# Second block: gate and heads copied out of PSUM by ACT, norm scales in the rotary tables, routing rows rounded in natural order

## The chip, the cores and the metric

The kernel runs on one core of one Trainium2 chip. A core has TensorE (PE, matrix products into PSUM), VectorE (DVE), ScalarE (ACT), GpSimd (POOL) and SyncE (SP, which here only issues DMAs); each works through its own instructions in order and waits on semaphores for the others. The metric is the device time of one execution in microseconds; for the kernel before it is the median of three runs.

## The reference

The function runs two transformer blocks on T = 256 tokens of width 1024, all in fp32. The first block has a feed-forward, a mixer of two attentions, a second feed-forward and a gated embedding stage. The second block, in which the change lies, is this (normalisations take a gain vector):

```python
h = rmsnorm(x, attn_norm)
q, k, v, iq, ik, iw, z, xbc, dt_raw, gate_a, gate_b = split(h @ w_in)
q = rope_partial(rmsnorm(q by 16 heads of 64, q_norm), pos)   # rope on the first 16 of 64 dims
k = rope_partial(rmsnorm(k by 4 heads of 64, k_norm), pos)
y_attn = dsa_attention(q, k, v, iq, ik, iw)                   # top-k of an index score, then softmax
xs, bs, cs = split(silu(causal_depthwise_conv(xbc)))
y_ssd = ssd_chunked(xs, dt, A, bs, cs) + d_skip * xs
y_ssd = gated_group_rmsnorm(y_ssd, z, ssd_norm)               # y * silu(z), then a norm by group
x = x + (sigmoid(gate_a) * (y_attn @ w_a) + sigmoid(gate_b) * (y_ssd @ w_s)) @ w_out
x = x + hier_moe(rmsnorm(x, ffn_norm))                        # 4 groups of 8 experts, two used per token
```

`rmsnorm(q, g)` is q times the reciprocal root of its mean square, times g. `rope_partial` rotates dims 0 to 7 against 8 to 15 with cos and sin and leaves 16 to 63 as they are.

## The kernel before

**Products.** An fp32 product is made of three products of rounded parts: hi by hi, hi by lo, lo by hi. Every chunk of weights comes as `raw` (1 MB DMAs from SP, four buffers), ACT rounds it to `hi` (L211) and DVE takes `lo` = raw - hi (L212); five pairs of hi and lo fit. So SP's DMAs wait for `lo` of an older chunk, ACT and DVE for a free pair, that is for PE, and PE for `lo`. PSUM has banks under the names `mm` (3), `o` (1), `at` (2) and `tp` (2); who reads a bank last decides when PE may write it again.

**Order.** The order of each engine's instructions is found when the program is built, by a list scheduler, except where the code says `keep`; POOL's is as written. On the chip each engine follows its list and cannot go round a wait.

**Second feed-forward (from about 405 to 575 us).** The input's norm is applied late: `by_token` (L398) makes two diagonal matrices of the tokens' scales (`diag`, L403, DVE), and PE's L404 multiplies them with a matrix of -1 to get the scales as a row, which DVE multiplies into the gate's half `sa` (L430). Products of this stage are L302 and L303. In the same stretch POOL issues the small DMAs of block 2's constants (`block2_consts`, lines 865 ff., helper L136 for a vector broadcast to all partitions) and of the routing (L1326 to L1335); DVE's L1400 multiplies a gain into the routing weights.

**Block 2 (from about 625 us).** `w_in`'s columns come by chunks in an order that weaves the gate `z`, the queries and `xbc` together. Queries and keys go through `heads_of`: DVE multiplies the PSUM bank by the broadcast gain into `q` or `k` (L954), ACT squares the bank (L956), DVE sums (L958), POOL takes the power -1/2 (L145) and DVE a Newton step (L153 to L156: `u`, `r`). Then DVE applies rope (L502 to L505) and PE transposes (L513). The gate's bank is read by ACT's tanh (L1242) and then by DVE, (tanh + 1) * z (L1243). DVE also runs the top-k on index scores in the same stretch (L1005 to L1019), and ACT the scores' relu (`rel`, L1002).

**End.** From about 972 us on SP streams 96 MB of expert weights (L1381, order kept) into 32 buffers and more of 512 KB, which become free as earlier stages finish; routing (`Route.feed`) runs meanwhile, and its rows are gathered per expert by products with a permutation matrix (L1465) that read the rounded rows `hfh` and `hfl` as weights.

## Time and profile before

| | us |
|---|---|
| median of three runs | 1232.69 (1232.3 to 1237.01) |
| the profiled execution | 1233.61 |
| its span | 1231.9 |
| PE busy | 1158.9 (94%) |
| DVE busy | 765.7 (62%) |
| ACT busy | 580.9 (47%) |
| POOL busy | 82.2 (7%) |

The profile is of one execution; times in it count from the start of its span. Busy times of matmuls include their pipelining, so a busy PE is not PE at its peak. A row of a timeline gives start and length in us, engine, line, operation, the tiles written and read, and in brackets how long the engine had been idle and what released it.

### The profile page before, as it was taken

What the parts mean: (1) busy time and instruction counts of PE and PEld (TensorE: products, weight loads), DVE (VectorE), ACT (ScalarE), POOL (GpSimd) and SP (SyncE); (2) the same over time, 40 slices, a digit from 0 to 9 for tenths busy, and PEclk for the clock granted to TensorE, in tenths of its full rate; (3) what the DMA queues carried; (4) which work ended last, traced back from release to release, by engine and by line L of the source; (5) the groups of instructions that cost most, each with busy time, mean ns of one, the idle gap of its engine ahead of it and who ended that gap; (6) DMA issues with size and microseconds to landing.
All of it is one profiled execution on the core that took longest, in us unless ns stands there. A gap on an engine that the chain in (4) does not pass through costs nothing.

```text
span 1231.9 us, 18388 instructions
## 1 busy us (share of the span) xinstructions
PE 1158.9 (94%) x7126; PEld 908.0 (74%) x7127; DVE 765.7 (62%) x1407; ACT 580.9 (47%) x947; POOL 82.2 (7%) x144
## 2 busy tenths in 40 slices
PE   6999999999999999999998899999999999787776
PEld 5888888977778788888876788898787875342432
DVE  6676748776447677664788777799786662121213
ACT  6555535456565556553654476666544431010100
POOL 2000001110000500000010200001010010000000
PEclk9999999999999999999999899999999999999999
DMA  9554754563334765475542444334754699999996
GB/s 344 185 202 122 255 173 147 176 200 125 120 113 151 195 201 178 135 253 199 176 169 71 171 138 138 137 103 141 188 184 155 220 416 418 418 417 419 418 419 252
DMA packets 106827, 266.23 MB, mean 216 GB/s; under 512 B 8692, under 2 KB 18592, under 8 KB 106736
## 3 DMA queue, kind: packets, MB, share of 16 engines
q1 hardware_dynamic: 104000, 259.45, 59.0%
q0 software_dynamic: 1728, 4.00, 1.4%
q10 hardware_dynamic: 1008, 1.57, 0.4%
q8 instruction: 57, 0.93, 0.3%
q14 instruction: 34, 0.28, 0.1%
HBM read 263.95 MB, written 1.05 MB: 215 GB/s over the span
## 4 chain that ended last, share of the span: by engine, by line
PE 55%; DMA 11%; DVE 8%; ACT 1%; POOL 1%; issue 1%; ACTq 0%; DVEq 0%; SPq 0%; POOLq 0%
PE mm L228 8%; PE mm L230 8%; PE mm L229 8%; DMA wq<-in_w_up_dram 4%; PE mm L302 3%; DMA wq<-in_w_gate_dram 2%; DVE lo L212 2%; PE at L302 2%; PE at L1579 2%; DMA wq<-in_w_down_dram 2%; PE mm L1632 2%; PE mm L1087 2%; PE mm L1088 1%; PE tp L302 1%; PE mm L1089 1%; PE mm L303 1%
## 5 line engine op out<-in xcount | busy, mean ns | idle before, releaser
L212 DVE TENSOR_TENSOR lo<-raw,hi 128x1024 fp32r<-128x1024 f32 (+3 forms) x312 | 366.0, 1180 | 179.5 <-ACT hi L211 175.0
L211 ACT CAST hi<-raw 128x1024 fp32r<-128x1024 f32 (+3 forms) x312 | 315.9, 1016 | 284.9 <-PE o L229 95.0
L302 PE MATMUL mm<-x,hi 128*128 128x512 f32 x272 | 100.4, 402 | 2.8 <-DVE x L184 2.8
L145 POOL TENSOR_TENSOR r<-ms,phalf 128x1 f32<-128x1 f32 (+2 forms) x40 | 40.9, 1024 | 723.3 <-DVE ms L143 718.1
L1579 PE MATMUL at<-wq,xg 128*32 128x256 f32 x736 | 66.9, 396 | 17.0 <-DMA wq<-in_w_up_dram 12.7
L228 PE MATMUL mm<-hi,xah 128*128 128x512 f32 x192 | 78.9, 412 | 2.6 <-DVE zs L1243 2.6
L303 PE MATMUL mm<-x,lo 128*128 128x256 f32 x272 | 76.5, 283 | 0.1
L229 PE MATMUL mm<-lo,xah 128*128 128x512 f32 x192 | 76.2, 397 | 0.2 <-DVE ms L143 0.2
L230 PE MATMUL mm<-hi,xal 128*128 128x512 f32 x192 | 76.1, 396 | 0.3 <-DVE xal L184 0.3
L302 PE MATMUL at<-x,hi 128*128 128x512 f32 x192 | 70.3, 392 | 0.0
L1579 PEld LDWEIGHTS at<-wq,xg 128*32 128x32 f32 x736 | 31.2, 112 | 46.4 <-DMA wq<-in_w_up_dram 23.0
L1589 DVE SCALAR_TENSOR_TENSOR act<-at,cg,sa 128x256 f32<-128x256 f32 x8 | 5.3, 665 | 94.3 <-ACT sa L1586 94.3
L302 PEld LDWEIGHTS mm<-x,hi 128*128 128x128 f32 x272 | 52.0, 192 | 15.3 <-DVE x L184 3.5
L1087 PE MATMUL mm<-xah,hi 128*128 128x256 f32 x192 | 57.7, 300 | 3.1 <-ACT sq L956 3.1
L302 PE MATMUL tp<-x,hi 128*128 128x512 f32 x160 | 59.0, 392 | 0.0
L1088 PE MATMUL mm<-xal,hi 128*128 128x256 f32 x192 | 55.9, 291 | 0.0
L1089 PE MATMUL mm<-xah,lo 128*128 128x256 f32 x192 | 55.4, 289 | 0.0
L1586 ACT ACTIVATE sa<-at,rs 128x256 f32<-128x256 f32 x8 | 3.8, 474 | 108.6 <-PE at L1579 74.4
L303 PE MATMUL at<-x,lo 128*128 128x256 f32 x192 | 53.5, 279 | 0.0
L303 PEld LDWEIGHTS mm<-x,lo 128*128 128x128 f32 x272 | 52.1, 193 | 0.8 <-DVE lo L212 0.8
L229 PE MATMUL mm<-lo,gxh 128*128 128x512 f32 x132 | 51.6, 391 | 0.0
L230 PE MATMUL mm<-hi,gxl 128*128 128x512 f32 x132 | 51.6, 391 | 0.0
(577 smaller groups left out, 2712.9 us busy)
## 6 DMA issues: line engine op xcount, KB each, us to landing
raw<-in_w_in_dram SPq DMA_DIRECT2D x50, 1024.0 KB, 4.9
raw<-in_ffn_w_in_dram SPq DMA_DIRECT2D x40, 1024.0 KB, 5.0
wq<-in_w_up_dram SPq DMA_DIRECT2D x48, 512.0 KB, 9.9
wq<-in_w_down_dram SPq DMA_DIRECT2D x48, 512.0 KB, 9.9
raw<-in_ffn_w_out_dram SPq DMA_DIRECT2D x22, 1024.0 KB, 5.0
wq<-in_w_gate_dram SPq DMA_DIRECT2D x44, 512.0 KB, 9.9
raw<-in_w_gate_dram SPq DMA_DIRECT2D x20, 512.0 KB, 10.0
raw<-in_w_out_dram SPq DMA_DIRECT2D x8, 1024.0 KB, 4.8
```

The costliest lines, as they stand in the source:

```text
L145: G.tensor_tensor(out=r0, in0=ms, in1=phalf[:, :n], op=ALU.pow)
L211: first(S.copy(hi, part))
L212: first(V.tensor_tensor(lo, part, hi.bitcast(F32), op=ALU.subtract))
L228: PE.matmul(ps, xh, wh, start=first, stop=False)
L229: PE.matmul(ps, xh, wl, start=False, stop=False)
L230: PE.matmul(ps, xl, wh, start=False, stop=last)
L302: PE.matmul(ps[f], hi[:, c, s], sx.both[k // 2][:, :, k % 2, :], start=(k == 0), stop=False)
L303: PE.matmul(ps[f][:, 1, :], lo[:, c, s], sx.hi(k), start=False, stop=(k == KC - 1))
L1087: PE.matmul(o, hi[:, c, s], xh, start=(k == 0 and f % 2 == 0), stop=False)
L1088: PE.matmul(o, hi[:, c, s], xl, start=False, stop=False)
L1089: PE.matmul(o, lo[:, c, s], xh, start=False, stop=(k == 7 and f % 2 == 1))
L1579: PE.matmul(pg[s, n * 256:n * 256 + 256], xg[k // 4][:, k % 4, c:c + CAP], ws[j][:, r * 256:r * 256 + 256], start=(n + k == 0), stop=(n + ...
```

## The change

1. `heads_of`: the multiplication by the gain (L954) goes. ACT copies the bank to `q` or `k` and then squares it; rope follows on the copy at once, with cos and sin tables that have the gain of the 16 rotated dims in them; the gain of the other 48 dims is applied by ACT when it takes the transposed heads out of PSUM, as a scale per partition (1 for the rotated dims).
2. The tables: eight products of 128x2x8 on DVE in the constants' second part. POOL's two broadcasts of 64 become two of 16 (`q_norm_rot`, `k_norm_rot`), two memsets and four DMAs of 48x1 (`..._rest`), all in the same place.
3. `on_z`: ACT copies the bank to `zs` and writes the tanh to a tile of its own; DVE's product reads both from SBUF.
4. `Route.feed`: the rows are rounded in natural order, one contiguous cast and one contiguous subtraction for each half of the tokens; PE then reads the gather's weights with a stride of eight elements. The first half's subtraction moves behind the permutation, as the second's was.

```diff
--- before.py
+++ after.py
...
-    def to_T(src, dst, n, width):
+    def to_T(src, dst, n, width, scale=None):
...
-            S.copy(dst[:width, j:j + m, :], p[:width, :m, :])
+            if scale is None:
+                S.copy(dst[:width, j:j + m, :], p[:width, :m, :])
+            else:
+                S.activation(dst[:width, j:j + m, :], p[:width, :m, :], AF.Identity, scale=scale[:width])
...
-        g_q = row_bcast(a["q_norm_2"], 64, "g_q2")
-        g_k = row_bcast(a["k_norm_2"], 64, "g_k2")
+
+        g_rot, g_rest = {}, {}
+        for nm in ("q_norm_2", "k_norm_2"):
+            g_rot[nm] = row_bcast(a[nm][:16], 16, nm + "_rot")
+            g_rest[nm] = cp.tile([128, 1], F32, name=nm + "_rest")
+            G.memset(g_rest[nm], 1.0)
+            for b in range(2):
+                G.dma_start(g_rest[nm][64 * b + 16:64 * b + 64, :], a[nm][16:64].rearrange("(p o) -> p o", o=1))
         g_ik = row_bcast(a["idx_k_norm_2"], 64, "g_ik2")
...
+        tabs = {}
+        for nm in g_rot:
+            c, n = [cp.tile([128, 2, 2, 8], F32, name=nm + z) for z in ("_c", "_s")]
+            g = g_rot[nm].rearrange("p (j d) -> p j d", j=2)
+            for j in range(2):
+                V.tensor_tensor(c[:, :, j], cs2[:, :, j], bc(g[:, None, j], [128, 2, 8]), op=ALU.mult)
+                V.tensor_tensor(n[:, :, j], sn2[:, :, j], bc(g[:, None, 1 - j], [128, 2, 8]), op=ALU.mult)
+            tabs[nm] = c, n, g_rest[nm]
+        g_q, g_k = tabs["q_norm_2"], tabs["k_norm_2"]
...
-        def heads_of(ps, n, gain, dst):
-
-            V.tensor_tensor(dst, ps.rearrange("p (h d) -> p h d", d=64), bc(gain[:, None, :], [128, n, 64]), op=ALU.mult)
+        def heads_of(ps, n, t, gain, dst):
+
+            S.copy(dst.rearrange("p h d -> p (h d)"), ps)
             sq = heap([128, n, 64], name="sq")
             S.activation(sq.rearrange("p h d -> p (h d)"), ps, AF.Square)
+            rope(dst[:, :, :16], gain[0][:, t], gain[1][:, t], n, 8)
             ss = small([128, n], name="ss")
             V.tensor_reduce(out=ss, in_=sq, axis=AX.X, op=ALU.add)
             return rstd(ss, n, 64)
...
-            rh = heads_of(ps[:, :256], 4, g_k, k)
-            rope(k[:, :, :16], cs2[:, t], sn2[:, t], 4, 8)
+            rh = heads_of(ps[:, :256], 4, t, g_k, k)
             kd = heap([128, 4, 2, 64], name="kd")
             V.tensor_tensor(kd, bc(k[:, :, None, :], [128, 4, 2, 64]), bc(rh[:, :, None, None], [128, 4, 2, 64]), op=ALU.mult)
-            defer(lambda: to_T(kd.rearrange("p h j d -> p (h j d)"), kT2[:, :, tok(t)], 4, 128), DEFK)
+            defer(lambda: to_T(kd.rearrange("p h j d -> p (h j d)"), kT2[:, :, tok(t)], 4, 128, g_k[2]), DEFK)
...
             q = heap([128, 8, 64], name="q2")
-            rh = heads_of(ps, 8, g_q, q)
+            rh = heads_of(ps, 8, t, g_q, q)
             V.tensor_scalar(sc_q[t][:, bi * 8:bi * 8 + 8], rh, 0.125, None, op0=ALU.mult)
-            rope(q[:, :, :16], cs2[:, t], sn2[:, t], 8, 8)
-            defer(lambda: to_T(q.rearrange("p h d -> p (h d)"), qT2[bi][:, :, tok(t)], 4, 128), DEFQ)
+            defer(lambda: to_T(q.rearrange("p h d -> p (h d)"), qT2[bi][:, :, tok(t)], 4, 128, g_q[2]), DEFQ)
...
         def on_z(t, bi, n0, nw, ps):
-            S.activation(zs[bi][:, t, :], ps, AF.Tanh, scale=0.5)
-            V.scalar_tensor_tensor(zs[bi][:, t, :], zs[bi][:, t, :], 1.0, ps, op0=ALU.add, op1=ALU.mult)
+            th = heap([128, 512], name="zth")
+            S.copy(zs[bi][:, t, :], ps)
+            S.activation(th, ps, AF.Tanh, scale=0.5)
+            V.scalar_tensor_tensor(zs[bi][:, t, :], th, 1.0, zs[bi][:, t, :], op0=ALU.add, op1=ALU.mult)
...
-            chunks = lambda z: z.rearrange("p (c q) -> p c q", c=8)
-            rows = h.rearrange("p (q c) -> p c q", c=8)
+            chunks = lambda z: z.rearrange("p (q c) -> p c q", c=8)
             self.hi[t], self.lo[t] = chunks(hh), chunks(hl)
-
-            def rest(c):
-                keep(V.tensor_tensor(self.lo[t][:, c], rows[:, c], self.hi[t][:, c].bitcast(F32), op=ALU.subtract))
-
-            keep(S.copy(self.hi[t], rows))
-            if t == 0:
-                rest(slice(0, 8))
-            else:
+            keep(S.copy(hh, h))
+            if t == 1:
                 self.first = self.gather(0, ("mm", "mm", "mm", "o"))
                 next(self.first)
             lg = heap([128, 40], name="lg")
             keep(V.scalar_tensor_tensor(lg, ps, r, br, op0=ALU.mult, op1=ALU.add))
             self.cw[t] = small([128, 4, 9], name="cw")
             G.tensor_copy(self.cw[t][:, :, 8:9], bc(r[:, None, :], [128, 4, 1]))
-            self.weigh[t] = self.choose(t, lg, lambda: [rest(slice(c, c + 4)) for c in (0, 4) if t])
+            self.weigh[t] = self.choose(t, lg, lambda: keep(V.tensor_tensor(hl, h, hh.bitcast(F32), op=ALU.subtract)))
```

DVE at the start of the second feed-forward, before. `wr` is the routing weights, `lo` a weight chunk's low part, `diag` what PE's L404 reads.

```order
L1400 TENSOR_TENSOR wr_3828<-wr_3828,g_col 128x320
L212 TENSOR_TENSOR lo_4012<-raw_4005,hi_4011 128x1024
L212 TENSOR_TENSOR lo_4050<-raw_4047,hi_4049 128x1024
L212 TENSOR_TENSOR lo_4054<-raw_4047,hi_4053 128x1024
L403 TENSOR_SCALAR diag_3936<-ident,r_3726 128x128
L403 TENSOR_SCALAR diag_3936<-ident,r_3811 128x128
L424 TENSOR_TENSOR sa_3987<-mm_3890,sa_3987 128x256
L424 TENSOR_TENSOR sa_3987<-mm_3891,sa_3987 128x256
L424 TENSOR_TENSOR sa_3994<-mm_3892,sa_3994 128x256
L212 TENSOR_TENSOR lo_4112<-raw_4109,hi_4111 128x1024
```

After (L1419 was L1400; L916 and L917 are the tables' products):

```order
L1419 TENSOR_TENSOR wr_3828<-wr_3828,g_col 128x320
L212 TENSOR_TENSOR lo_4020<-raw_4013,hi_4019 128x1024
L212 TENSOR_TENSOR lo_4058<-raw_4055,hi_4057 128x1024
L916 TENSOR_TENSOR q_norm_c<-cs_3840,q_norm_rot 128x2x8
L917 TENSOR_TENSOR q_norm_s<-sn_3841,q_norm_rot 128x2x8
L916 TENSOR_TENSOR q_norm_c<-cs_3840,q_norm_rot 128x2x8
L917 TENSOR_TENSOR q_norm_s<-sn_3841,q_norm_rot 128x2x8
L916 TENSOR_TENSOR k_norm_c<-cs_3840,k_norm_rot 128x2x8
L917 TENSOR_TENSOR k_norm_s<-sn_3841,k_norm_rot 128x2x8
L212 TENSOR_TENSOR lo_4062<-raw_4055,hi_4061 128x1024
L916 TENSOR_TENSOR k_norm_c<-cs_3840,k_norm_rot 128x2x8
L424 TENSOR_TENSOR sa_3995<-mm_3898,sa_3995 128x256
...
L424 TENSOR_TENSOR sa_4002<-mm_3900,sa_4002 128x256
L917 TENSOR_TENSOR k_norm_s<-sn_3841,k_norm_rot 128x2x8
L403 TENSOR_SCALAR diag_3944<-ident,r_3726 128x128
L403 TENSOR_SCALAR diag_3944<-ident,r_3811 128x128
```

`diag` stood fourth behind L1400 and now stands behind three `lo`, the eight products and three `sa`.

PE in the same place, before. L404 is the row of scales; `mm` and `o` are the first columns' products, `at` and `tp` the next ones.

```order
L302 MATMUL mm_3892<-x_755_3693,hi_3951 128x512
L303 MATMUL mm_3892<-x_755_3693,lo_3952 128x256
L302 MATMUL o_3893<-x_755_3693,hi_3951 128x512
L404 MATMUL at_3937<-diag_3936,neg_one 128x256
L303 MATMUL o_3893<-x_755_3693,lo_3952 128x256
L302 MATMUL at_4001<-x_752_3690,hi_4007 128x512
L303 MATMUL at_4001<-x_752_3690,lo_4008 128x256
L302 MATMUL tp_4003<-x_752_3690,hi_4007 128x512
```

After:

```order
L303 MATMUL mm_3900<-x_755_3693,lo_3960 128x256
L302 MATMUL o_3901<-x_755_3693,hi_3959 128x512
L303 MATMUL o_3901<-x_755_3693,lo_3960 128x256
L302 MATMUL tp_4011<-x_752_3690,hi_4015 128x512
L303 MATMUL tp_4011<-x_752_3690,lo_4016 128x256
L302 MATMUL tp_4012<-x_752_3690,hi_4015 128x512
L303 MATMUL tp_4012<-x_752_3690,lo_4016 128x256
L302 MATMUL tp_4011<-x_752_3690,hi_4015 128x512
L303 MATMUL tp_4011<-x_752_3690,lo_4016 128x256
L302 MATMUL tp_4012<-x_752_3690,hi_4015 128x512
L303 MATMUL tp_4012<-x_752_3690,lo_4016 128x256
L404 MATMUL at_3945<-diag_3944,neg_one 128x256
L302 MATMUL at_4009<-x_752_3690,hi_4015 128x512
```

L404 has moved behind the last `o` product and four pairs of the next columns.

DVE at the first two banks of queries, before. `sq` and `ss` are squares and sums; the first bank's tiles are q_1313 and ss_6401, the second's q_1322 and ss_6423.

```order
L954 TENSOR_TENSOR q_1313_6397<-mm_6303,g_q_3846 128x512
L502 TENSOR_TENSOR rope_1320_6413<-q_1313_6397,cs_3840 128x128
L504 TENSOR_TENSOR rope_1321_6414<-q_1313_6397,sn_3841 128x8x8 x2
L505 TENSOR_TENSOR q_1313_6397<-rope_1320_6413,rope_1321_6414 128x8x16
L954 TENSOR_TENSOR q_1322_6419<-mm_6304,g_q_3846 128x512
L958 TENSOR_REDUCE ss_6401<-sq_6399 128x8
L502 TENSOR_TENSOR rope_1329_6435<-q_1322_6419,cs_3840 128x128
L143 TENSOR_SCALAR ms_6403<-ss_6401 128x8
L504 TENSOR_TENSOR rope_1330_6436<-q_1322_6419,sn_3841 128x8x8 x2
L153 SCALAR_TENSOR_TENSOR u_6407<-r_1317_6405 128x8
L212 TENSOR_TENSOR lo_6588<-raw_6585,hi_6587 128x1024
L154 TENSOR_TENSOR u_6407<-u_6407,ms_6403 128x8
L505 TENSOR_TENSOR q_1322_6419<-rope_1329_6435,rope_1330_6436 128x8x16
```

After (q_1315 is the first bank, of the first half of the tokens, q_1324 the second):

```order
L502 TENSOR_TENSOR rope_1317_6425<-q_1315_6421,q_norm_c 128x128
L504 TENSOR_TENSOR rope_1318_6426<-q_1315_6421,q_norm_s 128x8x8 x2
L977 TENSOR_REDUCE ss_6431<-sq_6423 128x8
L505 TENSOR_TENSOR q_1315_6421<-rope_1317_6425,rope_1318_6426 128x8x16
L143 TENSOR_SCALAR ms_6433<-ss_6431 128x8
L153 SCALAR_TENSOR_TENSOR u_6437<-r_1321_6435 128x8
L212 TENSOR_TENSOR lo_6612<-raw_6609,hi_6611 128x1024
L154 TENSOR_TENSOR u_6437<-u_6437,ms_6433 128x8
L502 TENSOR_TENSOR rope_1326_6447<-q_1324_6443,q_norm_c 128x128
L156 SCALAR_TENSOR_TENSOR r_6440<-u_6437,r_1321_6435 128x8
L504 TENSOR_TENSOR rope_1327_6448<-q_1324_6443,q_norm_s 128x8x8
L993 TENSOR_SCALAR scq_5819<-r_6440 128x8
L504 TENSOR_TENSOR rope_1327_6448<-q_1324_6443,q_norm_s 128x8x8
L977 TENSOR_REDUCE ss_6453<-sq_6445 128x8
L505 TENSOR_TENSOR q_1324_6443<-rope_1326_6447,rope_1327_6448 128x8x16
```

The two rows L954 are gone; `u` (L153) follows `ms` directly, and the second bank's rope, which stood ahead of `u` but for its last step, now stands behind `u` and a `lo`.

## Rows read from the trace of the kernel before

**Rows 1.** Busy by stretch: PE, PEld, DVE, ACT, POOL (instructions); clock, DMA share, GB/s

```profile
400.00:425.00 25.00, 22.02 (x114) 18.31 (x113) 16.56 (x31) 13.73 (x25) 18.11 (x40) 0.93 0.68 169
425.00:450.00 25.00, 25.00 (x146) 22.04 (x145) 17.33 (x23) 14.20 (x22) 0.00 (x0) 1.00 0.67 226
650.00:675.00 25.00, 21.44 (x107) 16.20 (x106) 22.19 (x77) 11.77 (x19) 2.06 (x2) 0.95 0.25 84
700.00:725.00 25.00, 24.33 (x168) 21.72 (x169) 18.68 (x50) 15.60 (x37) 4.97 (x4) 0.87 0.37 126
1025.00:1050.00 25.00, 22.56 (x256) 13.23 (x248) 7.39 (x16) 3.72 (x8) 0.00 (x0) 1.00 1.03 418
```

**Rows 2.** SP in order of time from 925 to 1050: start, us, engine, line, operation

```profile
972.63 4.71 SPq L1381 DMA_DIRECT2D wq<-in_w_gate_dram  x8
```

**Rows 3.** What SP waited for from 930 to 1060: total us, times, longest

```profile
SPq L1381 <- DVE lo L212: 9.0, 1, 9.0
```

**Rows 4.** What PE waited for from 640 to 730: total us, times, longest

```profile
PE mm L1087 <- ACT sq L956: 3.1, 1, 3.1
PE mm L228 <- DVE zs L1243: 2.6, 1, 2.6
PE at L999 <- ACT rel L1002: 1.0, 1, 1.0
```

**Rows 5.** ACT in order of time; in brackets the idle time before and its releaser

```profile
656.24 0.39 ACT L956 ACTIVATE sq<-mm 128x256 f32<-128x256 f32 x1 [2.46 <-DVE k L954]
...
667.41 0.60 ACT L1242 ACTIVATE zs<-mm 128x512 f32<-128x512 f32 x1 [0.53 <-PE mm L230]
```

**Rows 6.** DVE in order of time in block 2

```profile
656.24 0.22 DVE L502 TENSOR_TENSOR rope<-k,cs 128x64 f32<-128x64 f32 x1
...
683.29 0.68 DVE L954 TENSOR_TENSOR q<-mm,g_q 128x512 f32<-128x512 f32 x1
...
688.16 0.17 DVE L153 SCALAR_TENSOR_TENSOR u<-r 128x8 f32<-128x8 f32 x1 [1.53 <-POOL r L145]
...
689.46 0.29 DVE L505 TENSOR_TENSOR q<-rope,rope 128x128 f32<-128x128 f32 x1
```

**Rows 7.** PE in order of time, one row at L404, one at L513

```profile
418.63 0.70 PE L404 MATMUL at<-diag,neg_one 128*128 128x256 f32 x2
...
689.37 1.15 PE L513 MATMUL tp<-ident,q 128*128 128x128 f32 x8
```

**Rows 8.** DVE in order of time at the start of the second feed-forward

```profile
413.12 0.50 DVE L1400 TENSOR_TENSOR wr<-wr,g_col 128x320 f32<-128x320 f32 x1 [6.11 <-DMA g_col<-in_ffn_norm_dram]
...
416.93 1.23 DVE L212 TENSOR_TENSOR lo<-raw,hi 128x1024 fp32r<-128x1024 f32 x1 [1.05 <-ACT hi L211]
418.07 0.50 DVE L403 TENSOR_SCALAR diag<-ident,r 128x128 f32<-128x128 f32 x2
418.47 1.08 DVE L424 TENSOR_TENSOR sa<-mm,sa 128x256 f32<-128x256 f32 x3
```

**Rows 9.** POOL in order of time, block 2's constants

```profile
411.88 0.54 POOL L1335 DMA_DIRECT2D br<-in_b_route_group_dram  x1 [0.29 <-POOL br L1333]
...
415.05 0.54 POOL L136 DMA_DIRECT2D g_q<-in_q_norm_dram  x1
...
417.16 0.54 POOL L136 DMA_DIRECT2D a_neg<-in_a_log_dram  x1
```

**Rows 10.** DMA issues from 404 to 426: tile, queue, KB each, median us to landing

```profile
sn<-in_c_sin_dram POOLq DMA_DIRECT2D x2, 8.0 KB, 2.7
...
b_dt<-in_dt_bias_dram POOLq DMA_DIRECT2D x1, 16.0 KB, 5.7
a_neg<-in_a_log_dram POOLq DMA_DIRECT2D x1, 16.0 KB, 6.9
```

**Rows 11.** The chain of waits from 990 to 1060: start, us, what

```profile
1029.74 4.10 PE mm L1465 x32
...
1038.80 9.93 DMA wq<-in_w_up_dram
```

More of the change, by code (lines that the diff above doesn't have):

```diff
@@ L65, in tile_blocks @@
     cp = ctx.enter_context(tc.tile_pool(name="consts", bufs=1))
-    cp.tile([128, 112], F32, name="pad")
+    cp.tile([128, 64], F32, name="pad")
     wp = ctx.enter_context(tc.tile_pool(name="weights", bufs=4))
```

## The prediction

> **What bounds the kernel now.** I read the table of busy time by stretch first, then PE's waits, then ACT, DVE and POOL in order of time around these waits, then the DMA rows and the chain of waits. TensorE is the engine that is always busy: 425 to 450 has 25.00 us of PE in 25, and most stretches up to 1000 read like it. The exceptions are what a change can win or lose. In [rows 1] the reader is to see 400 to 425 with 22.02 us of PE at a mean granted clock of 0.93, 650 to 675 with 21.44 at 0.95 and DVE at 22.19, and 700 to 725 at a clock of 0.87. From 1025 on the DMA share is 1.03 at 418 GB/s: the expert weights stream, and the end is the start of that stream plus a length that nothing here alters. Its first eight gate chunks go out at 972.63 [rows 2], and in that part SP stood 9.0 us behind a DVE `lo` for a weight buffer [rows 3]: buffers come free at the pace at which PE uses up the chunks. So what PE loses or wins before 972 moves the end one to one, and what comes later is hidden as long as the stream doesn't starve.
>
> **The edits in block 2, what they free.** Between 640 and 730 PE waits three times [rows 4]: 3.1 us at L1087 for ACT's `sq`, 2.6 at L228 for DVE's `zs`, 1.0 at L999 for `rel`, together 6.7 us. After such a wait the granted clock falls to its lower level for a while: a mean of 0.95 over 25 us is 1.25 us lost, 0.87 is 3.25 [rows 1]. With both, 11.2 us is the most that the edits can free there.
>
> All three have one cause, DVE's place in the release of PSUM. `sq` stands 2.46 us behind DVE's `k` at 656.24 [rows 5], because L954 has the bank first; and the gate's bank is held until DVE comes to L1243, though ACT was done with its tanh (0.60 us from 667.41) long before. Now ACT copies, squares and takes the tanh from banks that no DVE instruction reads. That adds 8 copies for `zs` and 4 for `q` at 0.60, and 2 for `k` at about 0.39, 8 us of ACT between 640 and 960. ACT is busy 11.77 and 15.60 of 25 us in the stretches of [rows 1], so I cost them at nothing; without that cover each copy ahead of a CAST would delay one `lo` by its 0.60 us, at most 8 us in all, a few of which PE would see.
>
> DVE sheds L954: four at 0.68 (about 0.60 net of overlap) and two half as wide, at about 0.35 [rows 6], 3.1 us in all. L1243 stays, now with SBUF operands; no row prices that form, and since L954 reads as much from PSUM in 0.68, I take it as unchanged, within 0.1 us a time.
>
> What is late next? The stretch is nearly DVE's: `lo`, top-k, the heads, and in between the wait for POOL's power (1.53 us at 688.16 [rows 6]). The number of `lo` ahead of the first softmax maximum stays, and so do the trips to POOL. In the new order `u` follows `ms` at once, and the second half's rope stands behind it and behind a `lo`. Before, that half's L505 ran at 689.46 [rows 6] and PE's transposes L513 began at 689.37 [rows 7], nearly in step. Without the wait at `zs` PE would come to L513 about 4 us earlier, at 685.4, while DVE's rope, shifted by hardly 1 us, ends near 688.5: a new wait of 3 us, with the clock's loss behind it, and some 0.6 us more for the `lo` behind top-k. In the end PE gains here what DVE gains. I take 3.3 us, the 3.1 us of L954 and a little for copies that start before DVE is free. Bounds: 1.0 us (only the wait for `rel` goes) and 11.2 us (all go and none comes).
>
> **The tables, what they cost.** The eight small products sit in the second part of the constants' code, and the order puts all eight near the start of the second feed-forward, ahead of `diag`, which PE's L404 needs; with them comes a wait for POOL's DMAs. Before, DVE ran `lo` at 416.93, `diag` at 418.07 [rows 8], and PE took L404 at 418.63 [rows 7] without a wait. Now DVE stops at the products until `k_norm_rot` has landed, and a `lo`, three `sa` and `diag` stand behind it. DVE doesn't go round a stall: at 413.12 it had stood 6.11 us for `g_col` [rows 8].
>
> When does it land? POOL issued `g_q` at 415.05 in 0.54 us [rows 9]; `q_norm_rot` takes that place. Then come a memset with a gap of 0.29, as ahead of the DMA at 411.88 [rows 9], and two column DMAs at 0.54: `k_norm_rot` goes out near 417.1. From issue to landing the rows give 2.7 us for `sn`, 5.7 for `b_dt` and 6.9 for `a_neg` [rows 10], the last issued at 417.16 [rows 9], while weights fill the DMA engines. `b_dt` has the same place in the queue, the fourth behind `sn`, so I take 5.7: landing 422.8, bounds 419.8 and 424.0.
>
> From there to `diag`: four products at 0.14 (L502 took 0.22 and the next began 0.14 later [rows 6]), a `lo` 1.14, three `sa` 1.08, two `diag` 0.50 [rows 8], 3.3 us: 426.1. PE's order has eight more matmuls ahead of L404, at 25.00/146 us each [rows 1] 1.4 us of work drawn forward, so it arrives at 420.0 and waits 6.1 us (bounds 3.1 and 7.3). The lower clock behind it costs more: the stretch 400 to 425, with 3.0 us without PE, lost 25 x 0.07 = 1.75 us by it, that of the 3.1 us wait 3.25 [rows 1, 4]. I take 2.0 (1.2 to 3.2). Sum 8.1 us, bounds 4.3 and 10.5. PE is full behind it, so none of it is made up.
>
> By the trace, then, a POOL DMA of a few KB lands after 2.7 us, or after 5.7 and more beside weight loads [rows 10]. The Trainium skill ("DMA: Bandwidth & Descriptors", section "Anatomy of one DMA — SWDGE (gpsimd) path") gives about 2.0 us of fixed cost for each transfer from this engine. By that the table would land at 419.1, PE would wait 2.4 us, and the term would be some 4 us instead of 8. No row shown is that short, and the sum goes by the rows.
>
> **The routing.** Rounding in natural order makes ACT's CAST and DVE's subtraction contiguous, some 1 us off a stretch that lies beneath the DMA stream; the gather's weights are then read with a stride of eight elements. One such group of 32 matmuls takes 4.10 us [rows 11]; no row shows strided loads, so their price lies between nothing and the same again. After it, at 1038.80, the chain goes over to the weights' DMA [rows 11], which runs ahead of PE by several buffers. I take 0, bounds -1 and +2.
>
> **The SSD part** is dealt anew, with `lo` somewhat earlier. PE waits there for nothing worth a row; 0, bounds 0 and +3.
>
> **Sum.** -3.3 + 8.1 + 0 + 0 = +4.8 us on the profiled execution's 1233.61 us, so 1238.4. That execution lay 0.9 us above the median of 1232.69; on the median's scale 1237.5.
>
> **Rivals.**
> 1. The tables at full price and little won in block 2 (slower). `k_norm_rot` takes `a_neg`'s 6.9 us and the clock costs 3.2: +10.5; block 2 gives 1.0 to 3.3 back. Net +7 to +9.5, 1240 to 1242. It decides from a landing after about 423.5. For it: `a_neg` was issued at the very time at which `k_norm_rot` will be. Against: `b_dt`, before it in the queue, took 1.2 us less.
> 2. The waits in block 2 really go (faster). The wait at L513 is short, since DVE's rope can start as soon as ACT has copied, and 9 to 11.2 us are won against 4.3 for the tables: -4.7 to -6.9, 1226 to 1228. For it: PE's three waits all name PSUM. Against: the stretch is nearly DVE's, which sheds only 3.1 us.
> 3. The tables cost little and block 2 is as forecast (no change): a landing near `sn`'s 2.7 us, 4.3 - 3.3 = +1, 1233.7. By the skill's fixed cost it would be this too. Against: beside the weights the rows took 5.7 and 6.9.
> 4. Strided weights slow the gather, or the new order starves PE in the SSD part: +3 on top of the forecast, 1240.5.
>
> **Chances.** Forecast 0.42 (some 0.04 of it beyond +6.2 us), rival 1 0.24, rival 2 0.17 (0.10 of it beyond -6.2 us), rival 3 0.12, rival 4 0.05. A measurement of this kernel tells about 0.5%, 6.2 us, from no change. So faster 0.10, same 0.57, slower 0.33. The range is 1227 to 1243: it takes in rivals 1, 3 and 4 and half of rival 2, and leaves out what lies beyond. The forecast's own range is 1234 to 1240.
>
> **What would show it.** Right: DVE stands idle for 6 to 7 us up to about 423, released by the DMA of `k_norm_rot`; PE waits about 6 us at L404 for `diag` and then runs at the lower granted clock; L1087, `zs` and `rel` are gone from PE's waits, one at L513 has come, and the expert stream begins near 977.5. Wrong: PE reaches 425 to 450 no later than before, or the stream's start moves by less than 1 us or more than 9.

## The result and the profile after

| | before | after |
|---|---|---|
| median us | 1233.06 (1232.0 to 1237.01, 6 runs) | 1241.51 (1240.58 to 1243.11, 6 runs) |
| profiled execution, its span | 1233.61, 1231.9 | 1240.58, 1238.9 |

The ratio of after to before is 1.0064, with a 95% interval of 1.0049 to 1.0080: slower by 0.64%, just past what can be told from no change. The time lies in the range of 1227 to 1243, 4.0 us above the forecast and above the forecast's own 1234 to 1240. No change (within 0.5%) had been given the best chance, and slower 0.33. The direction was right; three of the four sizes were not.

Busy time by stretch, after; the columns are those of [rows 1], with a stretch where the expert stream begins put in before the last:

```profile
400.00:425.00 25.00, 18.05 (x92) 14.81 (x90) 14.32 (x36) 10.92 (x21) 17.95 (x42) 0.93 0.57 141
425.00:450.00 25.00, 25.00 (x135) 21.88 (x136) 17.57 (x24) 15.41 (x23) 2.92 (x5) 0.93 0.63 203
650.00:675.00 25.00, 25.00 (x131) 19.68 (x130) 21.00 (x72) 15.31 (x28) 2.89 (x4) 1.00 0.37 126
700.00:725.00 25.00, 23.06 (x178) 20.00 (x178) 18.32 (x50) 16.78 (x36) 4.06 (x4) 1.00 0.38 127
1015.00:1035.00 20.00, 20.00 (x280) 13.36 (x283) 4.81 (x20) 4.29 (x10) 0.00 (x0) 0.90 0.98 365
1025.00:1050.00 25.00, 23.43 (x236) 16.64 (x235) 4.80 (x15) 4.39 (x8) 0.00 (x0) 0.93 1.02 394
```

Beside [rows 1], 400 to 425 has lost 4 us of PE and 425 to 450 now runs at 0.93. The stretches of block 2 are better: PE is full from 650 to 675, and the clock is 1.00 in both. The last two are worse: 394 GB/s where [rows 1] have 418.

DVE at the start of the second feed-forward, after (order of time, as [rows 8]), and below it POOL, PE and the DMAs of the same place:

```profile
414.42 2.35 DVE L212 TENSOR_TENSOR lo<-raw,hi 128x1024 fp32r<-128x1024 f32 x2
421.02 0.17 DVE L916 TENSOR_TENSOR q_norm_c<-cs,q_norm_rot 128x16 f32<-128x16 f32 x1 [4.25 <-DMA q_norm_rot<-in_q_norm_dram]
...
421.83 0.18 DVE L916 TENSOR_TENSOR k_norm_c<-cs,k_norm_rot 128x16 f32<-128x16 f32 x1 [0.36 <-DMA k_norm_rot<-in_k_norm_dram]
...
424.41 0.47 DVE L403 TENSOR_SCALAR diag<-ident,r 128x128 f32<-128x128 f32 x2
```

```profile
418.00 0.57 POOL L136 DMA_DIRECT2D k_norm_rot<-in_k_norm_dram  x1
```

```profile
424.93 1.00 PE L404 MATMUL at<-diag,neg_one 128*128 128x256 f32 x2 [4.03 <-DVE diag L403]
```

```profile
q_norm_rot<-in_q_norm_dram POOLq DMA_DIRECT2D x1, 8.0 KB, 4.9
k_norm_rot<-in_k_norm_dram POOLq DMA_DIRECT2D x1, 8.0 KB, 3.8
b_dt<-in_dt_bias_dram POOLq DMA_DIRECT2D x1, 16.0 KB, 3.3
```

The chain is the predicted one: the table's DMA, DVE's products, `diag`, PE at L404. `k_norm_rot` went out 0.9 us later than predicted (this execution was 1.0 us behind by then, see the ledger below) but took 3.8 us, not 5.7. DVE stood 4.25 us for `q_norm_rot` and 0.36 for `k_norm_rot`, and PE 4.03.

SP stood in the same place, because its next weight DMA needs a buffer that a `lo` behind DVE's products frees. Its wait for DVE from 404 to 430, by the row of DVE that came last:

```profile
SPq L202 <- DVE k_norm_c L916: 7.3, 1, 7.3
```

From 422 to 424 all DMAs together moved 22 GB/s in after, and 355 in late, a kernel of the experiments whose DVE doesn't stop there.

What PE waited for from 640 to 730, after (as [rows 4]), and DVE's two rows at the new wait:

```profile
PE tp L513 <- DVE ms L143: 3.0, 1, 3.0
PE mm L229 <- DVE lo L212: 1.1, 1, 1.1
PE tp L573 <- ACT prob L557: 1.1, 1, 1.1
PE tp L513 <- ACT hi L211: 0.5, 1, 0.5
```

```profile
691.83 0.17 DVE L153 SCALAR_TENSOR_TENSOR u<-r 128x8 f32<-128x8 f32 x1 [1.75 <-POOL r L145]
...
694.38 0.28 DVE L505 TENSOR_TENSOR q<-rope,rope 128x128 f32<-128x128 f32 x1
```

The three waits of [rows 4] are gone; the 3 us at L513 has come, behind the second half's rope, which stands behind `u`, as predicted.

In the SSD part, DVE and PE of after have a wait near 850 that before doesn't have, behind a DMA that POOL issues late. The rows of DVE, PE and POOL in after, and the last one's counterpart in before:

```profile
852.69 0.75 DVE L1252 SCALAR_TENSOR_TENSOR y<-y,r,g_ssd 128x512 f32<-128x512 f32 x1 [1.74 <-DMA g_ssd<-in_ssd_norm_dram]
```

```profile
853.49 0.66 PE L175 MATMUL tp<-ident,y 128*128 128x128 f32 x4 [1.69 <-DVE y L1252]
```

```profile
848.16 0.64 POOL L136 DMA_DIRECT2D g_ssd<-in_ssd_norm_dram  x1 [52.91 <-issue]
```

```profile
841.31 0.64 POOL L136 DMA_DIRECT2D g_ssd<-in_ssd_norm_dram  x1 [48.99 <-DVE conv L1055]
```

Before, the DMA was issued at 841.31, at a point of the program that after reaches 2.9 us later. So it comes about 4 us late for its place.

SP in order of time, after (as [rows 2]): the stream starts 4.75 us later, where 977.5 was predicted.

```profile
977.38 5.46 SPq L1400 DMA_DIRECT2D wq<-in_w_gate_dram  x8
```

And the chain of waits of after, later in the experts, where the same group as in [rows 11] takes twice the 4.10 us:

```profile
1089.90 7.95 PE mm L1477 x32
```

**The ledger.** The starts of the same matmuls were compared between two profiled executions; the table gives by how many us the median lag behind before (the 1233.61 execution) grew in each stretch. The stretches hold the constants' tables (400 to 600), block 2's heads and gate (600 to 740), the SSD part (740 to 900), and the routing and experts (900 to the end). "Tables late" means: the eight products stand in the constants' third part.

```
kernel           what it is                        to 400  -600   -740   -900   -end
after            all of the change                   0.96  +5.42  -3.50  +1.92  +2.28
late             after, tables late                  0.68  +0.58  -2.85  +1.87  +2.43
late_oldroute    late, routing as before             2.70  +2.51  -2.67  +2.08  -0.82
late2_oldroute   the same, tables behind wnl        -0.33  +1.77  -3.11  +2.02  -1.34
oldroute         after, routing as before            0.82  +5.54  -3.49  +2.07  +1.76
contig           after, gather reads contiguous      2.31  +5.76  -3.52  +1.90  -0.67
route_only       before + routing                    1.12  -1.10  -0.54  +0.03  +1.30
z_only           before + gate                       1.29  +0.65  -0.83  +2.05  -0.70
heads_only       before + heads, tables behind wnl   3.37  +1.70  -2.21  +0.05  -0.58
best_gsb4        late2_oldroute, g_ssd in 4 KB       0.32  +1.82  -3.18  +4.58  +2.23
best_gs0         late2_oldroute, first g_ssd 4 KB    0.35  +1.98  -3.18  +0.33  +0.11
nopool           late2_oldroute, no POOL power       3.13  -0.33 -11.18  +1.94  +0.12
before_again     before, unchanged                   1.09  -1.10  -0.59  -0.03  -1.33
```

The last row and the first column say how far executions lie apart with nothing changed: 0.6 to 1.3 us in a stretch behind 400 by the one; by the other, since up to about 395 us all kernels run the same instructions, -0.33 to 3.37 us. The last row is also a second yardstick: against that execution of before, after's 9.0 us are -0.1, +6.5, -2.9, +1.95 and +3.6.

### The profile page after: what moved, and what is told of

Its sections match the earlier page's. It is cut to its first block, busy times and chain, and to the rows that moved or that the text cites. A ratio compares the mean times of both kernels' runs of the same rounds, so it can differ in the third digit from the quotient of the medians.

```text
span 1238.9 us, 18418 instructions
## 1 busy us (share of the span) xinstructions
PE 1166.0 (94%) x7126; PEld 919.1 (74%) x7127; DVE 761.9 (62%) x1408; ACT 586.1 (47%) x961; POOL 82.8 (7%) x150
## 4 chain that ended last, share of the span: by engine, by line
PE 53%; DMA 14%; DVE 7%; POOL 2%; issue 1%; ACT 1%; ACTq 0%; DVEq 0%; SPq 0%; POOLq 0%
PE mm L228 8%; PE mm L230 8%; PE mm L229 8%; DMA wq<-in_w_up_dram 4%; DMA wq<-in_w_down_dram 2%; DMA wq<-in_w_gate_dram 2%; PE mm L302 2%; DVE lo L212 2%; PE at L302 2%; PE mm L1104 2%; PE mm L1105 2%; PE mm L1106 2%; DMA raw<-in_w_down_dram 2%; DMA raw<-in_w_gate_dram 2%; PE tp L302 1%
## 5 line engine op out<-in xcount | busy, mean ns | idle before, releaser
L302 PE MATMUL mm<-x,hi 128*128 128x512 f32 x272 | 100.8, 403 | 2.8 <-DVE x L184 2.8
L228 PE MATMUL mm<-hi,xah 128*128 128x512 f32 x192 | 78.6, 409 | 0.0
L303 PE MATMUL mm<-x,lo 128*128 128x256 f32 x272 | 76.8, 284 | 0.1
L1591 PE MATMUL at<-wq,xg 128*32 128x256 f32 x736 | 61.7, 383 | 12.8 <-DMA wq<-in_w_up_dram 9.0
L302 PE MATMUL at<-x,hi 128*128 128x512 f32 x192 | 71.6, 400 | 0.0
L302 PEld LDWEIGHTS mm<-x,hi 128*128 128x128 f32 x272 | 52.2, 192 | 15.3 <-DVE x L184 3.5
L302 PE MATMUL tp<-x,hi 128*128 128x512 f32 x160 | 59.0, 392 | 0.0
L1591 PEld LDWEIGHTS at<-wq,xg 128*32 128x32 f32 x736 | 28.4, 110 | 39.3 <-DMA wq<-in_w_up_dram 17.1
L303 PE MATMUL at<-x,lo 128*128 128x256 f32 x192 | 53.8, 281 | 0.0
L303 PEld LDWEIGHTS mm<-x,lo 128*128 128x128 f32 x272 | 52.5, 194 | 0.8 <-DVE lo L212 0.8
L228 PE MATMUL mm<-hi,gxh 128*128 128x512 f32 x132 | 51.4, 389 | 0.0
```

The lines of the kernel that those rows point to most:

```text
L228: PE.matmul(ps, xh, wh, start=first, stop=False)
L302: PE.matmul(ps[f], hi[:, c, s], sx.both[k // 2][:, :, k % 2, :], start=(k == 0), stop=False)
L303: PE.matmul(ps[f][:, 1, :], lo[:, c, s], sx.hi(k), start=False, stop=(k == KC - 1))
L1591: PE.matmul(pg[s, n * 256:n * 256 + 256], xg[k // 4][:, k % 4, c:c + CAP], ws[j][:, r * 256:r * 256 + 256], start=(n + k == 0), stop=(n + ...
```

## The experiments

The theory after the result: the 8.5 us between the medians are the tables (+5.5 to 6.5), block 2 (-3), the SSD part (+2) and the gather's strided weights (+2 to 3.5). The rivals: that the tables alone are the loss, that the SSD and late losses only follow from the shift, or that the routing's loss is its new order and not its stride.

**The tables.** Three kernels move the eight products past the feed-forward's start; in late they are all that moves on DVE, and the orders of PE and ACT stay.

```diff
-        tabs = {}            (second part of the constants)
...
         yield
+        tabs = {}            (third part; late: ahead of the split wnl)
...
+                keep(V.tensor_tensor(c[:, :, j], cs2[:, :, j], bc(g[:, None, j], [128, 2, 8]), op=ALU.mult))
+                keep(V.tensor_tensor(n[:, :, j], sn2[:, :, j], bc(g[:, None, 1 - j], [128, 2, 8]), op=ALU.mult))
```

> The changed kernel with one thing moved: the eight table products stand on DVE where the third part of block 2's constants is, some 180 DVE instructions later, far behind diag; nothing else changes place on DVE, PE or ACT. Theory (the tables ahead of diag cost 5.5 us of PE's time, 4.0 us of waiting at L404 and 1.5 us at the lower clock, and PE is full behind it): PE doesn't wait at L404, the lag of PE in the second feed-forward against the kernel before falls from 6.4 to about 0.9 us, and the time from 1241.5 to 1236.0. Rival (the lag is given back anyway further on, since DVE and the expert stream set the pace there): L404's wait goes but the time stays at 1240 to 1241.5.

Measured: 1237.56, ratio 1.0034 [1.0019, 1.0048], 1.6 above the theory's time and well below the rival's. In late's stretches the hole of after is gone, and the clock is at its upper level in both:

```profile
400.00:425.00 25.00, 22.08 (x121) 18.25 (x120) 17.04 (x32) 15.22 (x27) 16.70 (x38) 1.00 0.65 178
425.00:450.00 25.00, 25.00 (x143) 21.69 (x142) 17.48 (x23) 13.73 (x22) 4.11 (x9) 1.00 0.73 224
```

So the wait at L404 and the clock behind it are the tables', and they are worth 4.0 us of the time.

> Both repairs: tables late and the old routing; gate and heads still go out of PSUM by ACT. Theory (costs add up): 1241.5 - 5.5 - 2.3 = 1233.7, within 1.5 us of the kernel before, since block 2's gain of 3.5 us meets a loss of 1.9 near 850 and 0.9 that lies in the first microseconds of the execution. Rival (one of the two costs hides beneath the other): 1236 or more.

Measured: 1234.57, 1.0015 [1.0005, 1.0026], another 3.0 us less than late, from the routing, and 0.9 above the theory's sum.

> Gate and heads with both repairs, as the run with late tables and the old routing, but the products behind the split of the narrow weights instead of ahead of it. Theory (ahead of it they made PE's narrow products wait 0.6 us): that wait goes, the lag near 645 is 0.6 us less, time 1234.0. Rival: no difference, 1234.6.

Measured: 1234.75, 1.0017 [1.0001, 1.0032], as the rival has it: the place ahead of or behind `wnl` makes no difference.

**Block 2, part by part.**

```diff
 heads_only: heads_of, on_kv, on_q, to_T and the tables of after, all else of before
 z_only: on_z of after, all else of before
```

> The kernel before with the heads' part alone: ACT copies, tables scaled by the gains, their eight products put behind the split of the narrow weights so that nothing of the second feed-forward waits for them. Gate and routing as before. Theory (DVE sheds 3.1 us, the banks of q and k come free without DVE, the 2 KB buffers stay as they were): L1087's and rel's waits gone, no wait near 850, lag -2 to -3.5 us from 730 on, time 1230. Rival (the gain comes from the gate): lag within 1 us, time 1232 to 1233.

Measured: 1233.19, 0.9994 [0.9982, 1.0007], -2.2 us in the stretch, where before_again has -0.6 with nothing changed. The waits went as the theory said, but the time is the rival's and not 1230. What PE waited for from 640 to 730 in heads_only:

```profile
PE mm L228 <- DVE zs L1260: 3.6, 1, 3.6
PE tp L513 <- DVE ms L143: 2.0, 1, 2.0
```

> The kernel before with the gate's part alone (ACT copies the bank and writes the tanh to a tile of its own). Theory (the new tile moves the 2 KB buffers round by one, so that the first broadcast of the SSD norm's gain gets a buffer that a convolution leaves later, its DMA lands later, and DVE's product and PE's transposes near 850 wait 1.7 us; in block 2 the wait at zs goes, but DVE is as busy as before): L228's wait of 2.6 us is gone from 640 to 730, the lag there is -1 to -3, a new wait of 1.7 us at L175 near 850, time 1232 to 1234. Rival (the loss near 850 comes from the heads' new order): no wait near 850, time 1230 to 1231.

Measured: 1234.84, 1.0011 [0.9998, 1.0025], -0.8 us in the stretch, hardly more than before_again's -0.6, but +2.05 in the SSD part. The wait near 850 came as the theory said; the one at L228 didn't go. The same view of z_only, the first two rows:

```profile
PE mm L1087 <- ACT sq L956: 3.1, 1, 3.1
PE mm L228 <- ACT sq L956: 2.6, 1, 2.6
```

Alone, the gate's part changes nothing at L228 but the name of what is waited for: 2.6 us for `zs` in [rows 4], 2.6 for `sq` here. The heads alone leave the gate's wait. It takes both to free the banks, and then L513 is next.

What holds L513? In nopool the power for the heads' norms isn't taken on POOL.

```diff
-        G.tensor_tensor(out=r0, in0=ms, in1=phalf[:, :n], op=ALU.pow)
+        V.tensor_scalar(r0, ms, 0.25, None, op0=ALU.mult)      (block 2's heads alone)
```

> Gate and heads with late tables and the old routing, and in the heads' norm the trip to POOL for the power -1/2 replaced by a product on DVE (ms times a constant, so that the norm's value is wrong; the instructions behind it are the same). PE's and ACT's orders are unchanged. Theory (the gain in block 2 ends where DVE stands for POOL: PE waits 3 us at L513 because the second bank's rope is queued behind u, which waits for POOL): the waits at L513, 5.2 us in sum, fall below 1 us, the lag near 740 falls by another 3 to 5 us against the run with POOL's power, to about -5, time 1230 to 1231.5. Rival (DVE is full there anyway, and the wait is put down to the wrong instruction): lag within 1 us of that run, 1234 to 1235.

Measured: 1227.51, 0.9955 [0.9938, 0.9973], 7.2 us below late2_oldroute and 2.5 below the theory's 1230 to 1231.5. The same view of late2_oldroute and of nopool (its L516 is L513 of the others):

```profile
PE tp L513 <- DVE ms L143: 5.2, 2, 3.1
PE mm L229 <- DVE lo L212: 1.1, 1, 1.1
```

```profile
PE tp L516 <- ACT qT L520: 1.0, 1, 1.0
```

With PE's and ACT's orders unchanged, the waits go from 6.3 us to 1.0, and the stretch stands 11.2 us below before, the upper bound of the prediction's term. In late2_oldroute DVE stands idle for POOL's power six times in the heads, 1.0 to 1.8 us each and 8.8 in all; without these stops the stretch gains 8.1 us (11.18 - 3.11). So block 2's limit after the change is DVE's stop for POOL's answer and not the amount of DVE's work.

**The routing.** The stride alone, then the whole part, from both sides.

```diff
-            chunks = lambda z: z.rearrange("p (q c) -> p c q", c=8)      (contig)
+            chunks = lambda z: z.rearrange("p (c q) -> p c q", c=8)
...
 oldroute: Route.feed of before, all else of after; route_only: the reverse
```

> The changed kernel with only the view changed by which the gather's weights are read: 128 neighbouring elements instead of every eighth, so that experts get the columns in another order (the output is not the reference's). All engines' orders are those of the changed kernel. Theory (the stride costs): a group of 32 takes 4.1 us, the granted clock stays at 1.00 in 1035 to 1045, the time is about 1239.2, as with the old routing. Rival (not the stride but the later subtraction and the order of the products cost): groups stay near 8 us or the time near 1241.5.

Measured: 1240.06, 1.0060 [1.0044, 1.0076], between the theory's time and the rival's, and its interval overlaps that of after. So the time alone doesn't decide. All engines' orders are those of after. The gather's weight loads in after and then in contig, by shape (the mean ns of one stands behind the busy time):

```profile
L1477 PEld LDWEIGHTS mm<-perm,hfl 128*128 128x128 f32 x60 | 19.8, 339 | 0.0
```

```profile
L1477 PEld LDWEIGHTS mm<-perm,hfl 128*128 128x128 f32 x60 | 11.1, 191 | 0.1
```

The chain of contig has the group at 4.06 us:

```profile
1088.34 4.06 PE mm L1477 x32
```

A strided load takes 339 ns instead of 191, and the matmuls come at its pace. The stream at its start, in contig and in route_only:

```profile
1015.00:1035.00 20.00, 19.14 (x286) 13.76 (x286) 5.73 (x22) 4.38 (x11) 0.00 (x0) 1.00 1.03 417
```

```profile
1010.00:1030.00 20.00, 20.00 (x284) 13.32 (x284) 4.54 (x20) 4.28 (x10) 0.00 (x0) 0.93 0.98 375
```

After has 365 GB/s where contig has 417: over 20 us that is 20 x 52/417 = 2.5 us of stream, about the ledger's 2.28 - (-0.67) = 2.95. But after and contig differ there in the granted clock too, 0.90 and 1.00, and the next run shows that this matters.

> The changed kernel with the routing's rounding as before (permuted rows, contiguous weights, the first half's subtraction early). Theory (the strided weights double the gather's groups, 4.1 to 7.95 us, and let the expert stream starve once, about 2.3 us): the groups are back at 4.1 us, DMA stays at 418 GB/s from 1015 to 1035, the time is 1239.2. Rival (the gather lies beneath the stream, as predicted, and the 2.3 us come from the stream's start or the tail): groups of 4.1 us, time 1241 to 1242.

Measured: 1240.02, 1.0057 [1.0042, 1.0072], 1.5 us below after; the intervals overlap. The groups are back at 4.1 us, but the stream is not back at 418 GB/s, as the theory has it. Two stretches of oldroute:

```profile
1010.00:1020.00 10.00, 9.17 (x56) 8.59 (x56) 6.44 (x28) 2.49 (x10) 0.00 (x0) 0.55 1.02 410
1015.00:1035.00 20.00, 19.39 (x274) 13.07 (x278) 6.49 (x23) 4.29 (x10) 0.00 (x0) 0.90 0.97 365
```

With contiguous loads it has the 365 GB/s of after, and its profiled execution still lost 1.8 us at the end. What the two share is the clock, which fell near the routing: 0.55 from 1010 to 1020 here, 0.66 in after, 1.00 in contig. SP's longest wait for PE from 1000 to 1050, in after and then in oldroute, is much the same (in contig it is 3.1 us):

```profile
SPq L1400 <- PE at L1591: 6.6, 3, 5.7
```

```profile
SPq L1400 <- PE at L1598: 7.2, 4, 6.1
```

All fourteen profiled executions fit this. In seven the clock fell during the first gather: in after, late and route_only with the stride, in oldroute, best_gsb4, best_gs0 and nopool without it (in the last two only briefly). In just these the stream fell behind it, to between 252 and 361 GB/s in its worst 5 us; the other seven, none of them strided, had 408 or more throughout 1005 to 1040. The ledger's last column follows the clock as well: +1.3 to +2.4 with a long fall, +0.1 with a brief one, 0 or less without.

> The kernel before with the routing's part alone: natural order, strided weights. Theory (strided weights take twice as long, the first group pushes the experts' start back, and their buffers come free later): groups of 32 near 8 us, DMA below 418 GB/s for some 20 us after 1010, time 1.5 to 2.3 us above the kernel before, 1234.2 to 1235. Rival (the loss in the changed kernel came with the later stream's start): time within 0.5 us of the kernel before.

Measured: 1235.21, 1.0015 [1.0001, 1.0029], +1.8 us by the ratio, with nothing else changed. The routing part costs 1.5 to 3.0 us by the three pairs (oldroute, route_only, late against late_oldroute), all of the same sign, though the intervals of the first and the last pair overlap. How it costs them is not settled. That the stride doubles the group is shown; that the doubled group starves the stream is not, because no strided execution kept its clock, and a lower clock is followed by the same starving without the stride. All three strided executions fell and four of the eleven others, so the stride may bring the fall; that is argued and not shown.

**The SSD part.** z_only has the 2 us and heads_only has not, so it is the gate's. Its new tile `zth` has 2 KB, as `g_ssd` has, and it moves the 2 KB buffers round: `g_ssd` gets one that comes free later. Two kernels give it a buffer of 4 KB.

```diff
-                state["gs"] = row_bcast(a["ssd_norm_2"][g * 512:(g + 1) * 512], 512, "g_ssd", hp)
+                state["gs"] = heap([128, 1024], name="g_ssd")[:, :512]                   (best_gsb4)
+                state["gs"] = heap([128, 512 if g else 1024], name="g_ssd")[:, :512]     (best_gs0)
+                gap = a["ssd_norm_2"][g * 512:(g + 1) * 512]
+                G.dma_start(state["gs"], bass.AP(tensor=gap.tensor, offset=gap.offset, ap=[[0, 128], [1, 512]]))
```

> As the run before it, with the SSD norm's gain in one of the 4 KB buffers, whose last reader is done some 60 DVE instructions earlier; the order on all engines is the same. Theory (the DMA of that gain is late because of its buffer): DVE's 1.74 us wait for it and PE's 1.69 us at L175 near 850 go, time 1232.2, at or 1 us below the kernel before. Rival (PE is held there by DVE's backlog, and the wait moves to the next instruction): wait or lag stay, time 1234.

Measured: 1236.25, 1.0025 [1.0009, 1.0041], 1.5 above the median of late2_oldroute, which is the run it builds on; the intervals overlap, and its profiled execution is also one of those with a long fall of the clock. The first wait went, but the second `g_ssd` was late in its place, as DVE of best_gsb4 shows:

```profile
886.38 0.75 DVE L1254 SCALAR_TENSOR_TENSOR y<-y,r,g_ssd 128x512 f32<-128x512 f32 x1 [2.15 <-DMA g_ssd<-in_ssd_norm_dram]
```

> Gate and heads with late tables and the old routing, and only the first of the four broadcasts of the SSD norm's gain in a 4 KB buffer; the others in 2 KB buffers. Theory (each broadcast is as late as its buffer): neither the 1.7 us wait near 850 nor the 2.4 us wait near 887 shows, the lag stays near -1.5 from 740 to 970, time 1232 to 1233. Rival (the order, which differs in some 35 rows of DVE, brings a wait of its own): lag at 970 above 0, time 1234 or more.

Measured: 1232.96, 0.9992 [0.9977, 1.0007]. With the first `g_ssd` alone in a larger buffer the stretch costs 0.33 us instead of 2.02, and PE has no wait there. POOL's issue of it in late2_oldroute, and then in best_gs0:

```profile
843.60 0.64 POOL L136 DMA_DIRECT2D g_ssd<-in_ssd_norm_dram  x1 [52.89 <-issue]
```

```profile
815.91 0.64 POOL L1247 DMA_DIRECT2D g_ssd<-in_ssd_norm_dram  x1 [24.39 <-PE o L1223]
```

With the larger buffer the issue comes 28 us sooner and the wait goes: the cause is the buffer, not the gate's work. In both kernels the order of DVE and PE in the SSD part differs a little from late2_oldroute's (in best_gsb4 too, against its expectation), and the 0.33 us includes that. But the repaired kernel is as fast as before, not faster. Its ledger says why: -3.2 in block 2, and +2.0 already lost from 400 to 600, told of in the last section.

> The kernel before, unchanged, to see how much one program's stretches differ from one execution to the next. If the pitch of the feed-forwards' products (230 ns in one execution, a repeating 232, 241, 236 in others) and the clock's fall near 405 are a matter of the execution, one of them differs from the first profile; the first feed-forward, the same in all kernels, already had both pitches.

Measured: 1231.55, one run. Its stretch without the clock's fall that [rows 1] show at 400:

```profile
400.00:425.00 25.00, 21.60 (x119) 17.91 (x118) 17.50 (x32) 14.97 (x27) 18.49 (x38) 1.00 0.65 172
```

## Why the prediction was partly right

- **Block 2: the size right, its reason only in part.** -3.3 was predicted and -3.5 measured (-2.9 against before_again). The three waits went and the one at L513 came, 3.0 us where 3 was said, and ACT's copies cost PE no more than the 0.5 us at L513 that names `hi` (the 1.1 us for `prob` is DVE's, for whose `nb` ACT had itself stood 4.2 us). But "In the end PE gains here what DVE gains" takes DVE's work for the limit, and nopool shows that the limit is DVE's idle time behind POOL: with no less work on DVE the stretch gains 11.2 us. That is the gain of rival 2, whose condition didn't hold, since the rope waits its turn behind POOL's answer. (That nopool's time, 1227.5, also lies in the rival's 1226 to 1228 is chance: the rival has 4.3 us for the tables in it.)
- **The tables: the mechanism right, the size too large.** The step that failed is "so I take 5.7": the landing time of `k_norm_rot` was taken from `b_dt`'s place in the queue and was 3.8, and in the same execution `b_dt` fell from 5.7 to 3.3. PE waited 4.0 instead of 6.1, and the term was 5.4 (6.5 against before_again) instead of 8.1, inside its bounds. What 5.7 left out is that DVE's stop holds back `lo`, and so SP's weight DMAs, beside which the small ones land later: SP stood 7.3 us behind DVE there. `b_dt` landed in 3.0 to 3.3 us in the three kernels with early tables and in 5.3 to 6.5 in the seven with late ones. For `k_norm_rot` itself the two groups overlap (3.7 to 3.8, and 3.6 to 7.1), so for it this is likely but not shown. The clock's share was about right: 25 x 0.07 = 1.75 us from 425 to 450, where 2.0 was taken. (The order puts nine more matmuls ahead of L404, not eight; that is 0.2 us.) By the fixed cost of about 2.0 us of the Trainium skill ("DMA: Bandwidth & Descriptors", section "Anatomy of one DMA — SWDGE (gpsimd) path") the two tables would have landed sooner than they did: they took 4.9 and 3.8, and rival 3 fell.
- **The routing: wrong.** The step that failed is that the stream "runs ahead of PE by several buffers", and so hides what PE loses in the gather. At the start of the stream the buffers come free at PE's pace: SP stood up to 5.7 us behind PE, and 365 instead of 418 GB/s went through. Whether the stride or the lower clock slowed PE there stays open, since oldroute shows the same without the stride. By the times the price was at its upper bound, +2, or a little to either side of it (1.5 to 3.0).
- **The SSD part: wrong.** The step that failed is "PE waits there for nothing worth a row", true of before and no ground for after: a new tile in a pool shared by size moved another tile's DMA. +1.9 was within the bound of +3. Rival 4, at 0.05, had named both places, though for the SSD part it had a new order in mind and not a buffer.
- **The sum.** 5.4 - 3.5 + 1.9 + 2.3 + 1.0 (up to 400) = 7.1 on the profiled executions, 7.0 by their times, against 4.8 predicted. The 2.7 us too much for the tables hid most of the 4.2 us missing for routing and SSD, so the near miss owes something to luck. So does the stream's start at the predicted place: up to there 1.0 + 5.4 - 3.5 + 1.9 = 4.8, a sum of other terms. Nor does the time speak for rival 1, whose 1240 to 1242 it hits: `k_norm_rot` landed at 421.8 and not behind 423.5. The medians lie 8.5 apart: before's profiled execution lay 0.55 above its median, and after's, the fastest of its six, 0.93 below.

## What to carry to other kernels

A small table computed early for a late use puts its DMA's landing time into an in-order engine: place the product where the DMA has long landed. A new tile in a pool shared by size can delay a tile elsewhere, so list the buffers' neighbours by size before an edit is costed at nothing. A strided read of weights is paid on TensorE's load (339 ns instead of 191 here), and a stream that has slack later may have none in its first buffers. And compare the granted clock of two executions before a difference in their streams is put down to an edit.

## What the hardware showed unexpectedly

**The pace of identical matmuls.** In the feed-forwards one pair (L302, L303) takes 347 ns in some executions and 353 in others (means over some 200 pairs), at a granted clock of 1.00. PE of z_only, and then of late2_oldroute, in order of time, at the same place of the program:

```profile
520.41 0.40 PE L302 MATMUL tp<-x,hi 128*128 128x512 f32 x1
520.64 0.28 PE L303 MATMUL tp<-x,lo 128*128 128x256 f32 x1
```

```profile
519.63 0.40 PE L302 MATMUL tp<-x,hi 128*128 128x512 f32 x1
519.87 0.28 PE L303 MATMUL tp<-x,lo 128*128 128x256 f32 x1
```

The first pair's L303 starts 230 ns after its L302, the second's 240. From 432 to 528 this adds up to 1.84 us in each of the slower executions. In the second feed-forward all six kernels with late tables and POOL's power had the longer pace, while nopool (the same order there) and the kernels with early tables or with before's heads had not. In the first feed-forward, where all kernels run the same instructions, four executions had it: late_oldroute, contig, heads_only and nopool, those with 2.3 to 3.4 us in the ledger's first column. In the profiled executions it takes 1.84 of the tables' 6.5 us (against before_again) back from late, and most of block 2's gain from best_gs0; whether it is why the medians of after and late differ by only 4.0 isn't shown, since the pace of the other executions isn't on record. Its cause is open.

**The clock after short waits.** A wait of 2.1 us of PE at 405 was followed by a lower clock in one profiled execution of before (0.93 in [rows 1]) and not in the other (1.00 above), worth 1.1 us from 400 to 600 by the ledger. In after the clock was 0.60 in the first half of a strided group, where contig's whole group ran at 1.00 (0.12 us a matmul). Yet in after the matmuls came every 0.24 us at 0.60 and at 0.97 alike. The two halves of after's group, and then contig's group:

```profile
1090.00:1094.00 4.00, 4.00 (x17) 4.00 (x18) 0.41 (x2) 0.84 (x2) 0.00 (x0) 0.60 1.03 423
1094.00:1097.40 3.40, 3.40 (x16) 3.40 (x16) 0.69 (x1) 0.84 (x2) 0.00 (x0) 0.97 1.02 416
```

```profile
1088.30:1092.20 3.90, 3.86 (x32) 3.88 (x32) 1.25 (x3) 1.56 (x4) 0.00 (x0) 1.00 1.03 420
```

So in this group it is the load and not the clock that sets the pace.
